# One of the four sums of weight blocks of a feed-forward group, formed by an accumulating transfer instead of VectorE

## The chip, the core and the metric

The kernel runs on one core of a Trainium2 chip. Its time is the device time of one execution in microseconds (us); lower is better. A core has five engines with queues of their own: TensorE (PE; PEld is its loading of weights), VectorE (DVE), ScalarE (ACT), GpSimd (POOL) and SyncE (SP). The last two also issue transfers here. All transfers run on the core's 16 DMA engines.

## What is computed

One step of a decoder layer for 512 prompt tokens and 8 sampled tokens, 520 columns in all, with a model width of 2048: a mixer, a cross-attention and a feed-forward part, each added to the running sum. The change touches the feed-forward part alone:

```python
hf = rmsnorm(x, w['g_ffn'])
x = x + (jnp.square(jax.nn.relu(hf @ w['w_up'])) @ w['w_down']).astype(x.dtype)
```

`w_up` is 2048 x 8192 and `w_down` 8192 x 2048, both float32. After it comes one more normalisation, and the output is written.

## The kernel before

Every float32 matrix product is made of three products of rounded parts: a weight block is cast to a high part (`whi`, ScalarE, L128), and what the rounding left is formed as a low part (`wlo`, VectorE, L129); the activations are split in the same way. A weight block is a tile of 128 x 1024 float32 values, 512 KB. `whi` and `wlo` have three buffers each.

The work is a list of jobs, each with one block of weights. `run_jobs` (L163) gives every job's loads out five jobs ahead (`FETCH`), forms and splits its weights two jobs ahead (`w_split`), and then issues its matmuls. A scheduler with priorities sets the final order of the instructions on each engine; each engine then works its queue in order.

The feed-forward part replaces eight block products by seven (a scheme of Strassen's kind). `quad_jobs` makes the seven jobs of a group, P1, P2, P6, P5, P7, P3, P4 in this order (`ORDER`). A group has four blocks of weights, A11, A12, A21 and A22, and each block is 512 KB. From them four more blocks are formed on VectorE, all by `tt` (L1222):

- S3 = A11 - A21, for P7, formed with P1's weights;
- S1 = A21 + A22, for P5, formed with P6's weights and written over A21;
- S2 = S1 - A11, for P6, written over A11;
- A12 - S2, for P3, written over S2.

P1 multiplies A11, P2 multiplies A12 and P4 multiplies A22. `fetch0` loads A11 and A21, `fetch1` loads A12 and A22, all of them on SP's queue. A11 and A12 stand in tiles named `wraw` (three buffers), A21, A22 and S3 in tiles of a pool with five buffers; the trace leaves numbers out of names, so that A21 and A22 both read as `A` there, and S3 as `S`.

There are 63 groups: 31 of the up-projection (`up_quad`; its first block of columns is multiplied plainly), whose results go through the squared ReLU and are stored, split, to `hc`, 910 KB twice for each group; and 32 of the down-projection (`down_quad`), in eight rounds of four groups. Each round reads 28 blocks of hidden values (`ha`, 260 KB each) on SP's queue, fetched ahead. A result of a product is added from PSUM to the running sum X by VectorE. The last four groups of the down-projection have another order (`LATE_ORDER`: P1, P6, P5, P7, P3, P2, P4), and squares of the finished columns are summed beside them. After the last product the sums are scaled and stored; POOL multiplies some of them (L1430).

GpSimd's queue carries loads and stores of the mixer and of the attention until 1200 us, and then nothing but these multiplications at the end.

Of the kernel before, what the change touches and what calls it, by code (L numbers as in the profile page):

```python
# [12 lines left out]
ALU = mybir.AluOpType  # L13
# [32 lines left out]
def tile_trunk(ctx: ExitStack, tc: tile.TileContext, a, o):  # L46
    nc = tc.nc
    V, S, PE, G = nc.vector, nc.scalar, nc.tensor, nc.gpsimd
# [15 lines left out]
    def nm(s):  # L64
        uid[0] += 1
        return f"{s}_{uid[0]}"
# [13 lines left out]
    def mm_tile():  # L80
        return late.get("mm", pmm).tile([P, 2, 512], F32, tag="mm", name=nm("mm"))
# [23 lines left out]
    def w_raw(src):  # L105
        raw = wpool.tile([P, 8, P], F32, tag="wraw", name=nm("wraw"))
        load(raw, src)
        return raw
# [1093 lines left out]
    def quad_jobs(srcs, acts, nacc, evac, order=None):  # L1202


        q, ps = {}, {}

        def raw2(name, src=None):
            t = late["sb"].tile([P, 8, P], F32, tag="wq", name=nm(name), bufs=5)
            if src is not None:
                load(t, src)  # L1210
            return t

        def fetch0():
            q["A11"] = w_raw(srcs[0])
            q["A21"] = raw2("A21", srcs[2])

        def fetch1():
            q["A12"] = w_raw(srcs[1])
            q["A22"] = raw2("A22", srcs[3])

        def tt(out, u, v, op):
            V.tensor_tensor(out=out, in0=u, in1=v, op=op)  # L1222
            return out

        def form(p):
            if p == "P1":
                q["S3"] = tt(raw2("S3"), q["A11"], q["A21"], ALU.subtract)
                return q["A11"]
            if p == "P2":
                return q["A12"]  # L1230
            if p == "P6":
                q["S1"] = tt(q["A21"], q["A21"], q["A22"], ALU.add)
                q["S2"] = tt(q["A11"], q["S1"], q["A11"], ALU.subtract)
                return q["S2"]
            if p == "P3":
                return tt(q["S2"], q["A12"], q["S2"], ALU.subtract)
            return q[dict(P5="S1", P7="S3", P4="A22")[p]]

        def mm(p, wh, wl):
            acc = ACC[p]  # L1240
            if acc not in ps:
                ps[acc] = mm_tile()
            new = p in ("P1", "P2", "P5")
            blocks = acts(p)
            per = 8 // nacc
            for c in range(nacc):
                out = ps[acc][:, c, 0:HT]
                for k in range(per):
                    x = blocks[k]
                    j = c * per + k  # L1250
                    for wi, (w, b) in enumerate(((wh, 0), (wh, 1), (wl, 0))):
                        PE.matmul(out, w[:, j, :], x[:, b], start=(new and k == 0 and wi == 0),  # L1252
                                  stop=(p == LAST[acc] and k == per - 1 and wi == 2),
                                  skip_group_check=True)

        js = []
        for i, p in enumerate(order or ORDER):
            js.append(dict(fetch=(fetch0, fetch1, lambda: None)[min(i, 2)], form=lambda p=p: form(p),
                           cost=0.5, mm=lambda wh, wl, p=p: mm(p, wh, wl),
                           post=lambda p=p: evac(p, ps[ACC[p]])))  # L1260
        return js
# [349 lines left out]
```

## Time and profile before

| what | value |
|---|---|
| median of 3 runs | 2697.18 us (2695.01 to 2697.83) |
| the profiled execution | 2695.61 us, of it 2693.5 us from the first to the last instruction |
| granted TensorE clock, mean | 0.997 of full speed |
| bytes moved by transfers | 512.41 MB, mean 190 GB/s |
| feed-forward groups of seven products | from about 1407 us to 2678 us |

Shares and rows below belong to the profiled execution. A row of a timeline gives the start in us from the span's start, the duration in us, the engine, the line of the program, the operation, the tile written and the tiles read with their shapes, and a count; in brackets at its end, where there are any, stand the idle time of the engine ahead of it and what ended that. A row of busy time by stretch gives the stretch, its length, the busy us (and instructions) of PE, PEld, DVE, ACT and POOL, the granted TensorE clock, the DMA share and GB/s. A DMA share is the mean busy share of the 16 DMA engines. Queue q0 carries the transfers that POOL issues, q1 those of SP.

### The profile page before, as it was taken

The numbers are of one execution on the slowest core, as the hardware profiler recorded it, in microseconds if no ns is written. First come the engines' busy times: TensorE is split into PE (matmuls) and PEld (weight loads), VectorE is DVE, ScalarE is ACT, GpSimd is POOL, SyncE is SP. The second block draws the span as 40 slices with busy tenths as digits, with TensorE's granted clock in tenths as the row PEclk, the third lists the DMA queues.
The fourth block names the chain that finished last, engine by engine and source line by source line (L and its number), as shares of the span: only waits on it lengthen the run. The fifth ranks groups of instructions, "written<-read, shape, count | busy, mean of one in ns | idle before, by whom it ended". The sixth has DMA issues, their size and how long they took to land.

```text
span 2693.5 us, 52716 instructions
## 1 busy us (share of the span) xinstructions
PE 2664.7 (99%) x21586; PEld 2628.1 (98%) x21586; DVE 2052.9 (76%) x3447; ACT 1219.4 (45%) x1653; POOL 152.1 (6%) x288
## 2 busy tenths in 40 slices
PE   9999999999999999999999999999999999999997
PEld 9999999999999998989999999999999999999997
DVE  6786686853345567875559899999999898898898
ACT  5646355542233135444445555555554333333344
POOL 0011010000001322210000000000000000000001
PEclk9999999999999999999999999999999999999999
DMA  5364353534435777876566656656569766556542
GB/s 202 105 189 138 119 166 104 171 95 139 138 130 197 259 269 248 277 244 203 183 213 213 229 186 203 203 186 205 202 213 337 239 214 220 171 169 206 206 133 89
DMA packets 225923, 512.41 MB, mean 190 GB/s; under 512 B 25502, under 2 KB 91710, under 8 KB 225682
## 3 DMA queue, kind: packets, MB, share of 16 engines
q1 hardware_dynamic: 205074, 441.92, 49.3%
q0 software_dynamic: 20608, 67.13, 7.4%
q8 instruction: 170, 2.79, 0.4%
q14 instruction: 71, 0.58, 0.1%
HBM read 416.16 MB, written 92.94 MB: 189 GB/s over the span
## 4 chain that ended last, share of the span: by engine, by line
PE 92%; DVE 3%; DMA 2%; ACT 1%; issue 1%; POOL 0%; SPq 0%; POOLq 0%; ACTq 0%; DVEq 0%
PE mm L1252 46%; PE mm L201 36%; PE aux L220 2%; PE mm L981 2%; PE mm L1012 2%; DMA wraw<-in_w_mv 1%; PE mm L1296 1%; DVE wlo L129 1%; DMA wraw<-in_w_mk 1%; DVE wlo L145 0%; PE aux L728 0%; ACT whi L128 0%; DMA out_rh<-hs 0%; PE aux L657 0%; ACT whi L137 0%
## 5 line engine op out<-in xcount | busy, mean ns | idle before, releaser
L128 ACT CAST whi<-wraw 128x1024 fp32r<-128x1024 f32 x396 | 416.0, 1050 | 807.4 <-PE mm L1252 376.4
L1252 PE MATMUL mm<-ha,whi 128*128 128x260 f32 x3584 | 643.7, 283 | 1.6 <-ACT whi L128 1.0
L129 DVE TENSOR_TENSOR wlo<-wraw,whi 128x1024 fp32r<-128x1024 f32 x396 | 484.2, 1223 | 198.7 <-ACT whi L128 196.0
L1252 PEld LDWEIGHTS mm<-ha,whi 128*128 128x128 f32 x3584 | 551.0, 188 | 2.4 <-ACT whi L128 1.2
L1252 PE MATMUL mm<-ha,wlo 128*128 128x260 f32 x1792 | 505.1, 282 | 0.6 <-DVE wlo L129 0.6
L1252 PE MATMUL mm<-ta,whi 128*128 128x260 f32 x1984 | 359.1, 283 | 0.0
L1252 PEld LDWEIGHTS mm<-ha,wlo 128*128 128x128 f32 x1792 | 337.0, 188 | 1.0 <-DVE wlo L129 1.0
L1252 PEld LDWEIGHTS mm<-ta,whi 128*128 128x128 f32 x1984 | 305.3, 188 | 0.0
L1252 PE MATMUL mm<-ta,wlo 128*128 128x260 f32 x992 | 280.1, 282 | 0.0
L1252 PE MATMUL mm<-fa,whi 128*128 128x260 f32 x1488 | 270.3, 283 | 0.0
L201 PE MATMUL mm<-xh,whi 128*128 128x260 f32 x1280 | 264.0, 287 | 0.0
L201 PE MATMUL mm<-xl,whi 128*128 128x260 f32 x1280 | 259.5, 284 | 0.0
L201 PE MATMUL mm<-xh,wlo 128*128 128x260 f32 x1280 | 257.7, 282 | 0.0
L1252 PEld LDWEIGHTS mm<-fa,whi 128*128 128x128 f32 x1488 | 229.2, 188 | 0.0
L137 ACT CAST whi<-wraw 128x1024 fp32r<-128x1024 f32 x100 | 105.0, 1050 | 256.3 <-PE mm L201 92.3
L128 ACT CAST whi<-A 128x1024 fp32r<-128x1024 f32 x126 | 132.2, 1049 | 185.9 <-PE mm L1252 125.5
L1252 PE MATMUL mm<-fa,wlo 128*128 128x260 f32 x744 | 210.0, 282 | 0.0
L1361 DVE TENSOR_TENSOR X<-mm,X 128x260 f32<-128x260 f32 x448 | 170.9, 422 | 40.5 <-PE mm L1252 39.4
L201 PEld LDWEIGHTS mm<-xh,whi 128*128 128x128 f32 x1280 | 198.4, 188 | 1.3
L201 PEld LDWEIGHTS mm<-xh,wlo 128*128 128x128 f32 x1280 | 198.1, 189 | 0.2
L201 PEld LDWEIGHTS mm<-xl,whi 128*128 128x128 f32 x1280 | 197.8, 189 | 0.3
L1252 PEld LDWEIGHTS mm<-ta,wlo 128*128 128x128 f32 x992 | 186.7, 188 | 0.0
(397 smaller groups left out, 5249.0 us busy)
## 6 DMA issues: line engine op xcount, KB each, us to landing
ha<-hc SPq DMA_DIRECT2D x224, 260.0 KB
wraw<-in_w_in SPq DMA_DIRECT2D x80, 512.0 KB
wraw<-in_w_up SPq DMA_DIRECT2D x66, 512.0 KB
wraw<-in_w_down SPq DMA_DIRECT2D x64, 512.0 KB
A<-in_w_down SPq DMA_DIRECT2D x64, 512.0 KB
A<-in_w_up SPq DMA_DIRECT2D x62, 512.0 KB
hc<-hhi SPq DMA_DIRECT2D x32, 910.0 KB
hc<-r SPq DMA_DIRECT2D x32, 910.0 KB
```

Of the source, the lines that this page charges most:

```text
L128: S.copy(hi, raw)
L129: V.tensor_tensor(out=lo, in0=raw, in1=hi.bitcast(F32), op=ALU.subtract)
L137: S.copy(hi, raw)
L201: PE.matmul(ps[:, hf, 0:HT], w[:, j, :], x[:, HALF[hf]], start=(k == 0 and wi == 0), stop=(k == n - 1 and wi == 2))
L220: PE.matmul(out, u, v, start=first and i == 0, stop=last and i == 2)
L981: PE.matmul(box["ps"], w[:, i, :], x, start=(k == 0 and wi == 0), stop=(k == KB - 1 and wi == 2))
L1012: PE.matmul(box["ps"][:, i], x[:, ms], w[:, j], start=(k == 0 and wi == 0), stop=(k == KB - 1 and wi == 2))
L1252: PE.matmul(out, w[:, j, :], x[:, b], start=(new and k == 0 and wi == 0), stop=(p == LAST[acc] and k == per - 1 and wi == 2), skip_group_c ...
L1296: PE.matmul(ps[:, hf, 0:HT], w[:, j, :], x[hf][:, b], start=(kp == 0 and j == 0 and wi == 0), stop=(kp == 1 and j == 7 and wi == 2))
L1361: V.tensor_tensor(out=x, in0=c, in1=x, op=ALU.add)
```

## The change

S1 is no longer an addition on VectorE. Once S3 has been formed, GpSimd issues a transfer that reads A22 from HBM and adds it to A21 in SBUF; S1 is the same tile as before. The load of A22 on SP's queue stays as it is, because P4 multiplies A22 itself.

```diff
         def form(p):
             if p == "P1":
                 q["S3"] = tt(raw2("S3"), q["A11"], q["A21"], ALU.subtract)
+                q["S1"] = q["A21"]
+                G.dma_start(q["S1"], srcs[3], accum_op=ALU.add)
                 return q["A11"]
             if p == "P2":
                 return q["A12"]
             if p == "P6":
-                q["S1"] = tt(q["A21"], q["A21"], q["A22"], ALU.add)
                 q["S2"] = tt(q["A11"], q["S1"], q["A11"], ALU.subtract)
                 return q["S2"]
```

VectorE's order in an early group of the up-projection, before, from S3 to S2 (`S3_2285` is the S3 of this group, `A21_2274` and `A22_2279` are its blocks, `wraw_2273` is A11 and then S2; L1327 to L1335 work on the results, L1280 on the hidden values):

```order
L1222 TENSOR_TENSOR S3_2285_16868<-wraw_2273_16764,A21_2274_16766 128x1024
L1327 TENSOR_TENSOR r_2269_16727<-mm_2272_16737,r_2269_16727 128x260
L129 TENSOR_TENSOR wlo_2276_16769<-S3_2261_16634,whi_2275_16768 128x1024
L1269 SCALAR_TENSOR_TENSOR r_2269_16727<-r_2269_16727,rssf_2211_16250 128x260
L1280 TENSOR_TENSOR r_2245_16493<-r_2245_16493,hhi_2277_16772 128x1820
L129 TENSOR_TENSOR wlo_2281_16808<-wraw_2249_16530,whi_2280_16807 128x1024
L1222 TENSOR_TENSOR A21_2274_16766<-A21_2274_16766,A22_2279_16804 128x1024
L129 TENSOR_TENSOR wlo_2284_16838<-A22_2255_16570,whi_2283_16837 128x1024
L129 TENSOR_TENSOR wlo_2287_16871<-wraw_2273_16764,whi_2286_16870 128x1024
L1335 TENSOR_TENSOR r_2269_16727<-r_2269_16727 128x260
L1222 TENSOR_TENSOR wraw_2273_16764<-A21_2274_16766,wraw_2273_16764 128x1024
```

The same piece of VectorE's order with the change:

```order
L1222 TENSOR_TENSOR S3_2285_16868<-wraw_2273_16764,A21_2274_16766 128x1024
L1328 TENSOR_TENSOR r_2269_16727<-mm_2272_16737,r_2269_16727 128x260
L129 TENSOR_TENSOR wlo_2276_16769<-S3_2261_16634,whi_2275_16768 128x1024
L1270 SCALAR_TENSOR_TENSOR r_2269_16727<-r_2269_16727,rssf_2211_16250 128x260
L1281 TENSOR_TENSOR r_2245_16493<-r_2245_16493,hhi_2277_16772 128x1820
L129 TENSOR_TENSOR wlo_2281_16808<-wraw_2249_16530,whi_2280_16807 128x1024
L129 TENSOR_TENSOR wlo_2284_16838<-A22_2255_16570,whi_2283_16837 128x1024
L129 TENSOR_TENSOR wlo_2287_16872<-wraw_2273_16764,whi_2286_16871 128x1024
L1336 TENSOR_TENSOR r_2269_16727<-r_2269_16727 128x260
L1222 TENSOR_TENSOR wraw_2273_16764<-A21_2274_16766,wraw_2273_16764 128x1024
```

The addition that wrote A21 is gone, and all else stands in the same order; the last row, S2, reads what the transfer leaves in A21. Over the whole program 63 such rows leave VectorE; of the rest a handful change places with a neighbour.

POOL's order at the end of the attention, before (the last loads, then the end of the kernel, L1430):

```order
L864 DMA kv_1977_14113<-in_V 128x512
L864 DMA kv_1978_14114<-in_V 128x512
L1430 ISA
L1430 TENSOR_TENSOR y_3962_31546<-X_3019_23807,rf_3955_31520 128x260
L1430 TENSOR_TENSOR y_3963_31550<-X_3045_24048,rf_3955_31520 128x260
```

And with the change:

```order
L864 DMA kv_1977_14113<-in_V 128x512
L864 DMA kv_1978_14114<-in_V 128x512
L1229 DMA A21_2182_16080<-in_w_up 128x1024
L1229 DMA A21_2250_16532<-in_w_up 128x1024
L1229 DMA A21_2274_16766<-in_w_up 128x1024
L1229 DMA A21_2298_17000<-in_w_up 128x1024
L1229 DMA A21_2322_17234<-in_w_up 128x1024
```

63 transfers, 31 of `w_up` and 32 of `w_down`, now stand between the attention's loads and the multiplications at the end. On SP's queue no transfer is added or removed; in some groups a weight load trades places with a neighbouring load.

## Rows read from the trace of the kernel before

**Rows 1.** The page, busy time (share of the span), instructions.
```profile
PE 2664.7 (99%) x21586; PEld 2628.1 (98%) x21586; DVE 2052.9 (76%) x3447; ACT 1219.4 (45%) x1653; POOL 152.1 (6%) x288
```

**Rows 2.** Busy time by stretch (columns as told above): up-projection, end.
```profile
1700.00:1850.00 150.00, 150.00 (x1254) 150.00 (x1253) 136.63 (x172) 81.05 (x97) 0.00 (x0) 1.00 0.61 205
...
2600.00:2693.00 93.00, 79.46 (x645) 77.68 (x644) 80.68 (x143) 43.84 (x73) 8.40 (x12) 0.95 0.29 98
```

**Rows 3.** Waits of TensorE, 1400 to 2640 us: total, times, longest.
```profile
PE mm L1252 <- ACT whi L128: 1.0, 1, 1.0
PE mm L1252 <- DVE X L1361: 0.5, 1, 0.5
PE mm L1252 <- DVE wlo L129: 0.4, 1, 0.4
```

**Rows 4.** Timeline of VectorE, one up group: S3, S1, P1's low half, S2, P2's, P6's.
```profile
1694.70 1.22 DVE L1222 TENSOR_TENSOR S<-wraw,A 128x1024 f32<-128x1024 f32 x1
...
1700.75 1.22 DVE L1222 TENSOR_TENSOR A<-A,A 128x1024 f32<-128x1024 f32 x1
...
1704.28 1.23 DVE L129 TENSOR_TENSOR wlo<-wraw,whi 128x1024 fp32r<-128x1024 f32 x1 [1.17 <-ACT whi L128]
...
1705.76 1.22 DVE L1222 TENSOR_TENSOR wraw<-A,wraw 128x1024 f32<-128x1024 f32 x1
...
1707.57 1.22 DVE L129 TENSOR_TENSOR wlo<-wraw,whi 128x1024 fp32r<-128x1024 f32 x1
...
1710.07 1.23 DVE L129 TENSOR_TENSOR wlo<-wraw,whi 128x1024 fp32r<-128x1024 f32 x1 [0.57 <-ACT whi L128]
```

**Rows 5.** Groups of POOL by line: busy us, mean ns of one.
```profile
L864 POOL DMA_DIRECT2D kv<-in_V x64 | 34.5, 539 | 29.0 <-DVE od L900 13.5 <-DVE sc L893 7.2 <-DMA kv<-in_V 3.2
```

**Rows 6.** Timeline of VectorE, one down group: S3, S2, P2's low half.
```profile
2319.19 1.23 DVE L1222 TENSOR_TENSOR S<-wraw,A 128x1024 f32<-128x1024 f32 x1
...
2330.42 1.22 DVE L1222 TENSOR_TENSOR wraw<-A,wraw 128x1024 f32<-128x1024 f32 x1
...
2332.23 1.22 DVE L129 TENSOR_TENSOR wlo<-wraw,whi 128x1024 fp32r<-128x1024 f32 x1
```

**Rows 7.** Timeline of VectorE, one of the last four groups: S3, S2.
```profile
2623.27 1.22 DVE L1222 TENSOR_TENSOR S<-wraw,A 128x1024 f32<-128x1024 f32 x1
...
2634.39 1.22 DVE L1222 TENSOR_TENSOR wraw<-A,wraw 128x1024 f32<-128x1024 f32 x1
```

**Rows 8.** Timeline of ScalarE: P5's cast in both groups, P2's at a handover.
```profile
1711.89 1.05 ACT L128 CAST whi<-A 128x1024 fp32r<-128x1024 f32 x1 [0.88 <-PE mm L1252]
...
2336.73 1.05 ACT L128 CAST whi<-A 128x1024 fp32r<-128x1024 f32 x1 [1.82 <-PE mm L1252]
...
2371.11 1.05 ACT L128 CAST whi<-wraw 128x1024 fp32r<-128x1024 f32 x1 [1.82 <-PE mm L1252]
```

**Rows 9.** Transfers issued 940 to 946 us: count, size, median us to landing.
```profile
kv<-in_K POOLq DMA_DIRECT2D x3, 256.0 KB, 3.7
```

**Rows 10.** Transfers issued 1047 to 1060 us.
```profile
kv<-in_K POOLq DMA_DIRECT2D x8, 256.0 KB, 7.2
```

**Rows 11.** Busy time by stretch: those loads, the first handover, a later one.
```profile
1047.00:1064.00 17.00, 16.57 (x84) 13.68 (x83) 12.89 (x36) 6.68 (x10) 7.52 (x14) 1.00 1.00 372
2010.00:2130.00 120.00, 118.96 (x993) 118.64 (x992) 109.42 (x151) 49.37 (x49) 0.00 (x0) 1.00 0.94 325
2337.00:2371.00 34.00, 34.00 (x286) 34.00 (x286) 30.63 (x44) 12.34 (x12) 0.00 (x0) 1.00 0.95 339
```

**Rows 12.** The page, DMA queue of SP: packets, MB, share of 16 engines.
```profile
q1 hardware_dynamic: 205074, 441.92, 49.3%
```

**Rows 13.** Busy time by stretch, the same up group.
```profile
1696.00:1698.00 2.00, 2.00 (x19) 2.00 (x18) 2.00 (x4) 1.85 (x2) 0.00 (x0) 1.00 0.00 0
1698.00:1700.00 2.00, 2.00 (x19) 2.00 (x19) 2.00 (x2) 0.76 (x2) 0.00 (x0) 1.00 0.90 307
```

**Rows 14.** Timeline of SP, a later handover: the load of A12.
```profile
2357.58 0.33 SPq L107 DMA_DIRECT2D wraw<-in_w_down  x1
```

## The prediction

> **What bounds the kernel now.** I read the share of busy time first, then busy time by stage, then the waits of TensorE, then the engines' timelines over single groups of seven products, and last the transfers. TensorE is busy for 99% of the span [rows 1]. By stage it is busy for all 150 us of a stretch of the up-projection, beside 136.63 us of VectorE and a DMA share of 0.61; only in the last 93 us does it stand still for longer, and most of that is the final normalisation and the store of the output [rows 2]. From 1400 to 2640 us its named waits come to 1.0 + 0.5 + 0.4 = 1.9 us in all [rows 3]. So the feed-forward stage runs at the pace of the matmuls. VectorE is nearly full there, but it runs ahead of TensorE by the depth of the buffers, and nothing waits for it.
>
> **What the change takes away.** 63 additions of 1.22 us on VectorE (the middle row of [rows 4] is one): 76.9 us of busy time. What hides them is TensorE. With them gone, VectorE comes sooner to its next wait, for the cast of a block, which itself waits for TensorE to give back a buffer (the 1.17 us ahead of 1704.28 grow) [rows 4]. Gain: at most the 1.9 us of [rows 3], and likely none of it, since those three waits do not follow an addition. I take 0.
>
> **What it adds.** 63 transfers on POOL's queue. Each can begin only when S3 has been read off the old A21, and the same 512 KB of A22 are read from HBM a second time: the plain load on SP stays, since P4 multiplies A22 itself. So 33 MB more are read from HBM, and the sum's destination is read and written in SBUF. Issuing one of the 256 KB transfers took POOL 539 ns [rows 5]; POOL does nothing else in this stage, the next sum's transfer comes a group (20 us) later, and the twelve multiplications that end the kernel stand behind the last. POOL's queue I cost at nothing.
>
> **What waits for it.** VectorE now waits for the transfer just ahead of S2 = S1 - A11, and everything behind S2 on VectorE is held with it. The cover has two parts.
>
> First, S3 to S2. In an up group S3 ends at 1694.70 + 1.22 = 1695.92 and S2 begins at 1705.76: 9.84 us [rows 4]. In a down group 2319.19 + 1.23 = 2320.42 to 2330.42: 10.0 us [rows 6]. In one of the last four groups, with their other order, 2623.27 + 1.22 = 2624.49 to 2634.39: 9.9 us [rows 7].
>
> Second, what is queued behind S2. The low half of P2's block ends at 1707.57 + 1.22 = 1708.79 [rows 4], and TensorE takes up P2 only at 1711.89. That I read from the casts: there are three buffers, so the cast for the product two places later begins when P2 does [rows 8]. So 3.1 us more may pass before TensorE stands still. In a down group it is 2336.73 - (2332.23 + 1.22) = 3.3 us [rows 6, 8]. A delay of that size does not pile up from group to group: VectorE has 0.57 us, 1.17 us and the 1.22 us saved, 2.96 us in each group, to catch up. In the last groups VectorE is full, so there I count no second part.
>
> So the cover is **12.9 us** in the 31 up groups, 13.3 us in the down groups and 9.9 us in the last ones, from the end of S3 to the landing.
>
> **How long the transfer takes.** No row shows an adding transfer. From below: a plain 256 KB load on POOL's queue among little other traffic landed in 3.7 us [rows 9], as if size and addition cost nothing. From above: the same kind of load in a stretch where the DMA share was 1.00 landed in 7.2 us [rows 10, 11]; four times that, for twice the bytes with a destination that is read as well, is 28.8 us, if all of it were bytes. Between them: 512 KB cost all 16 engines together 0.493 x 2693.5 us / 441.92 MB x 0.524 MB = 1.58 us [rows 12]. An adding transfer reads 1 MB where the row of 3.7 us read 256 KB, three quarters of a megabyte more, 2.4 us. Quiet: 0.5 + 3.7 + 2.4 = 6.6 us. Against a full queue, with half of the engines' turns: 0.5 + 7.2 + 2 x 2.4 = 12.5 us. In an up group the transfer begins near 1696.5, when the DMA engines are idle, and meets the group's own stores and loads from 1698 on [rows 13]. I take **9 us**, between the two: it lands at about 1704.9, before S2. Both values lie inside 12.9 us, so the term is 0 with either; the quiet value also holds for most down groups and the last ones.
>
> One rule of the Trainium skill speaks against the change: SBUF — State Buffer, section "SBUF: two separate sides". A transfer issued from GpSimd has its descriptors written by GpSimd, and these writes stand still while a VectorE operation holds the port pair that the two share. By the rule the transfer would start only when VectorE pauses, and the sum would be the third rival's. The page's section "Who interferes with whom" says that the two-tensor form, which is what VectorE runs in this stage, has no such mode. No run here shows an adding transfer beside a full VectorE.
>
> **What it does to the other transfers.** A group's adding transfer reads 512 KB from each of two places: 2 x 1.58 = 3.2 us of all engines [rows 12] in 20 us, which adds 0.16 to a share of 0.61 [rows 2]: room enough. It is tight only where the next hidden blocks are fetched, 34 us at 0.95 in each of the later handovers and 120 us at 0.94 at the first [rows 11]. In the later ones a weight load issued at 2357.58 [rows 14] is first cast at 2371.11 [rows 8]: 13.5 us. If it landed as quickly as the load of [rows 9], 9.8 us are to spare; if it landed only as the burst ends, near 2371, none. I take 8 us of room against a delay of some 5 us, so 0.
>
> **The sum.** 2695.61 us (the profiled execution: span 2693.5 us and 2.1 us around it), less 0, plus 0. The median of the three runs stands 1.57 us above that execution, so the forecast is **2697.2 us**, no change. A measurement of this kernel can tell some 0.2%, 5.4 us, from no change; the forecast's own range is that, 2692 to 2702.
>
> **The rivals.**
>
> 1. Slower: the transfer lands after the cover in the up groups, where it shares the engines with two stores of 910 KB and three loads [rows 13]. It decides from 12.9 us after S3 on. At 14 us the cost is 1.1 us x 31 = 34 us, **2731 us**; at the upper bound, (28.8 - 12.9) x 63, about 1000 us. For it: the loaded estimate is already 12.5 us. Against it: the head start in idle engines, and that 7.2 us belongs to a stretch with several such loads in flight, where here there is one.
> 2. Slower: the full stretches at the handovers. Two transfers of 3.2 us meet 0.05 x 34 = 1.7 us of room, so loads fall 4.7 us behind; at the first, six of them, 19 us against 7, 12 us behind. Weight loads then come after their cast. With 1 us lost at each of the seven and 5 us at the first: 12 us, **2709 us**; at most 7 x 4.7 + 12 = 45 us. Against it: the 9.8 us to spare above.
> 3. Slower: VectorE holds up the start. In an up group it pauses first at 1703.1 (1704.28 less 1.17) [rows 4]; 9 us later is 1712.1, 6.3 us late for S2 and 3.2 us beyond the cover: 31 x 3.2 = 100 us, **2797 us**. Against it: VectorE runs two-tensor forms alone here.
> 4. Faster by more than 5.4 us: there are 1.9 us of waits to remove [rows 3], so this needs something that no row shows.
>
> That the addition does not leave VectorE can be excluded: its 63 rows are gone from VectorE's order and stand in POOL's.
>
> **How the numbers follow.** Forecast 0.68; late landing 0.17; handovers 0.10; VectorE's hold 0.03; faster 0.02. So faster 0.02, same 0.68, slower 0.30. The range goes from 2692, the lower edge of no change, to 2731, the first rival at 14 us; it leaves out about half of that rival, the third and most of the fourth, 0.13 in all.
>
> **What would show it.** Right: no rows of VectorE that add A22 to A21, VectorE's busy time 77 us lower, 63 more transfers of 512 KB on POOL with a median landing near 9 us, S2 waiting for them seldom and by less than 3 us, and TensorE's waits in the stage still near 2 us. Rival 1 shows as idle time ahead of S2 in each up group, released by the transfer, with TensorE waiting for low halves; rival 2 as TensorE's waits only near the handovers; rival 3 as landings that follow VectorE's pauses. The forecast is wrong if a landing passes 13 us in the ordinary groups.

## The result and the profile with the change

| | before | with the change |
|---|---|---|
| median | 2697.51 us (14 runs, 2695.01 to 2699.45) | 2703.29 us (14 runs, 2700.9 to 2709.56) |
| ratio | | 1.0023, 95% interval 1.0016 to 1.003 |
| profiled execution, its span | 2695.61 us, 2693.5 us | 2700.9 us, 2699.1 us |

The change costs 0.23%, 5.8 us. That is inside the range and just past the bound of no change. All ratios leave out executions over 1.5% above the fastest of the same kernel; there was one, of 8946.21 us, in the run below in which VectorE adds in 5 groups, with a mean granted clock of 0.285.

Busy time by engine [rows 1]:

```profile
PE 2667.2 (99%) x21586; PEld 2630.2 (97%) x21586; DVE 1989.0 (74%) x3384; ACT 1218.9 (45%) x1653; POOL 206.9 (8%) x351
```

VectorE has 63 instructions fewer, and 63.9 us less busy time where the prediction said 77. Added up one by one, the durations of its instructions do fall by 77.8 us. The rest is overlap: an instruction that follows another at once starts some 0.08 us before that one's end, and busy time counts this stretch once. With the additions gone more of the others come after a pause (879 instead of 793), and 13.9 us less of them overlap. TensorE is busy for 2.5 us longer with the same instructions, which points to its clock.

The two stretches of [rows 2], and the crowded one of [rows 11]:

```profile
1700.00:1850.00 150.00, 150.00 (x1254) 150.00 (x1254) 128.23 (x164) 81.07 (x97) 6.08 (x7) 1.00 0.81 229
2600.00:2693.00 93.00, 84.61 (x688) 82.75 (x686) 82.23 (x146) 45.73 (x75) 10.20 (x14) 0.99 0.34 99
2010.00:2130.00 120.00, 116.19 (x949) 115.71 (x948) 99.27 (x139) 47.56 (x48) 5.20 (x6) 0.97 1.00 340
```

In an ordinary stretch TensorE is as full as before, and the DMA share went from 0.61 to 0.81. The end holds more of TensorE's work only because everything arrives there 5 us later. At the first handover, from the up- to the down-projection, the share is 1.00, TensorE lost 2.8 us of busy time, and the mean granted clock is 0.97.

TensorE's waits from 1400 to 2640 us [rows 3], and VectorE's for transfers in the same part:

```profile
PE mm L1253 <- DVE X L1362: 3.7, 2, 3.1
PE mm L1253 <- ACT whi L128: 0.7, 1, 0.7
```

```profile
DVE wraw L1222 <- DMA A<-in_w_down: 3.8, 3, 1.8
...
DVE X L1362 <- DMA X<-dx: 3.4, 1, 3.4
```

S2 (`wraw`, L1222) waited for the new transfer in three of 63 groups, none of the up-projection. One addition to X waited 3.4 us for a plain load of X. The new transfers by themselves, from the rows of `A` on POOL, with POOL's DMA queue (before, it took 7.4%):

```profile
L1229 POOL DMA_DIRECT2D A<-in_w_down x32: 857/867/891, 2018.7 to 2650.4; - x32
L1229 POOL DMA_DIRECT2D A<-in_w_up x31: 856/867/908, 1379.0 to 1998.5; - x31
...
DMA to landing us min/median/max: 5.3/5.7/11.0
```

```profile
q0 software_dynamic: 29680, 100.16, 14.7%
```

A transfer lands in 5.7 us in the median, in 7.8 us for those of `w_down` alone. It takes (0.147 x 2699.1 - 0.074 x 2693.5) / 63 = 3.1 us of all 16 engines.

### The profile page after: what moved, and what is told of

Read it like the earlier page. It is cut to its first block, busy times and chain, and to the rows that moved or that the text cites. A ratio compares the mean times of both kernels' runs of the same rounds, so it can differ in the third digit from the quotient of the medians.

```text
span 2699.1 us, 52928 instructions
## 1 busy us (share of the span) xinstructions
PE 2667.2 (99%) x21586; PEld 2630.2 (97%) x21586; DVE 1989.0 (74%) x3384; ACT 1218.9 (45%) x1653; POOL 206.9 (8%) x351
## 4 chain that ended last, share of the span: by engine, by line
PE 92%; DVE 2%; DMA 2%; issue 2%; ACT 1%; POOL 0%; SPq 0%; POOLq 0%; DVEq 0%; ACTq 0%
PE mm L1253 44%; PE mm L201 36%; PE mm L981 3%; PE aux L220 2%; PE mm L1012 2%; PE mm L1297 1%; DVE wlo L129 1%; PE aux L728 1%; PE aux L657 0%; DMA hc<-r 0%; DMA out_rh<-hs 0%; PE aux L661 0%; ACT whi L128 0%; PE aux L654 0%; PE aux L252 0%
```

## Where the time went

The chain that ended last, of before and then of the change, in order of time (start, duration, what):

```profile
1407.05 635.54 PE mm L1252 x5302
2042.62 1.05 ACT whi L128
2043.86 564.23 PE mm L1252 x4715
```

```profile
1407.00 610.15 PE mm L1253 x5092
2017.14 5.02 DMA ha<-hc
2022.16 12.60 DMA hc<-r
2034.83 5.22 DMA X<-dx
2040.08 0.43 DVE X L1362
...
2042.71 5.37 PE mm L1253 x23
2048.10 1.05 ACT whi L128
2049.18 564.23 PE mm L1253 x4715
```

Both reach the seven-product groups at 1407 us, and both run without a break for the same 564.23 us after the first handover, through all seven later ones. Between them the change lost (2049.18 - 1407.00) - (2043.86 - 1407.05) = **5.37 us, once**. Below, "the stage" is the time from the start of that first run of matmuls to the end of the last: 2043.86 + 564.23 - 1407.05 = 1201.04 us before, 1206.41 us with the change. It leaves out the attention, which wanders by some us from one execution to the next.

What happened there, on TensorE (its two breaks) and by stretch:

```profile
2042.71 0.80 PE L1253 MATMUL mm<-ha,whi 128*128 128x260 f32 x2 [3.12 <-DVE X L1362]
2049.18 0.48 PE L1253 MATMUL mm<-ha,whi 128*128 128x260 f32 x2 [0.69 <-ACT whi L128]
```

```profile
2039.00:2043.00 4.00, 0.88 (x6) 0.67 (x6) 2.91 (x6) 2.08 (x2) 0.00 (x0) 0.89 1.01 385
2043.00:2048.00 5.00, 5.00 (x24) 5.00 (x24) 3.19 (x3) 0.58 (x1) 0.87 (x1) 0.50 1.05 371
```

TensorE stood still for 3.12 + 0.69 us, where before it stood for 1.04 us, so 2.8 us are stops. The other 2.6 us go with the clock: after the long stop the granted clock was 0.50, its lower level of 1.2 GHz, for five us, in which 24 matmuls ran instead of some 42. Before, the stop of 1.04 us was followed by no such stretch.

The queue of SP ahead of it, before and then with the change:

```profile
2022.33 7.09 SPq L1353 DMA_DIRECT2D ha<-hc  x7
2031.35 2.14 SPq L1381 DMA_DIRECT2D X<-dx  x4
```

```profile
2023.72 9.11 SPq L1354 DMA_DIRECT2D ha<-hc  x7
2034.83 2.27 SPq L1382 DMA_DIRECT2D X<-dx  x4
```

X is issued 3.5 us later, and VectorE waits 3.4 us for it, so it had hardly any room. An estimate says the same: 5.22 us from issue to landing (the chain of the change), put after 2031.35, gives 2036.57, and before, VectorE's first addition to X began at 2036.63.

## The experiments

The theory after the first reading: the whole loss is made at the first handover, because the adding transfers' share of full DMA engines makes X late. Its rivals: a loss too thin to see, spread over 63 groups; and the waits of S2 in later down groups. All ratios are against runs of the kernel before on the same chip. The stage is read from one profiled execution of each kernel; in the three that lost nothing it agrees to 0.03 us (1201.04, 1201.02 and 1201.03 us).

| run | median, us | ratio (95%) | the stage, us, against 1201.04 |
|---|---|---|---|
| VectorE adds in 2 groups | 2699.74 | 1.0008 (0.9999 to 1.0017) | 1202.82, +1.78 |
| transfer in 2 groups alone | 2700.6 | 1.0015 (1.0007 to 1.0024) | 1204.87, +3.83 |
| X's first loads on POOL | 2703.19 | 1.0023 (1.0013 to 1.0033) | 1207.88, +6.84 |
| copy without a wait in 2 groups | 2699.18 | 1.0007 (0.9998 to 1.0016) | +0.43 (to the last break) |
| VectorE adds in 5 groups | 2698.16 | 1.0003 (0.9994 to 1.0012) | 1201.02, -0.02 |
| plain load in place of the sum | 2699.24 | 1.001 (1.0001 to 1.0019) | 1203.10, +2.06 |

### Take the transfer away at the handover, and keep it there alone

`quad_jobs` got a switch for each group; with it off, VectorE adds as before:

```diff
             if p == "P1":
                 q["S3"] = tt(raw2("S3"), q["A11"], q["A21"], ALU.subtract)
-                q["S1"] = q["A21"]
-                G.dma_start(q["S1"], srcs[3], accum_op=ALU.add)
+                if moved:
+                    q["S1"] = q["A21"]
+                    G.dma_start(q["S1"], srcs[3], accum_op=ALU.add)
...
             if p == "P6":
+                if not moved:
+                    q["S1"] = tt(q["A21"], q["A21"], q["A22"], ALU.add)
```

First run: `moved=i != 31` in `up_quad`, `moved=(ck, g) != (0, 0)` in `down_quad`.

> 61 transfers as in the changed kernel; only the last up group and the first down group form S1 by VectorE's addition. Theory (all of the loss is made once, at the first handover, by the engine time of the two transfers issued there at 1998 and 2019 us): X's first loads go out near 2031 us again, TensorE's long stop there goes from 3 us to 1 us, the granted clock stays at 1.00, and the time is that of the kernel before, 2697.5 us within 1.5 us. Rival 1 (the loss is spread over the 63 groups, too little in each to be seen as a named wait): some 61/63 of it stays, about 2703. Rival 2 (VectorE's three waits of 3.8 us for adding transfers in down groups cost it): these groups are left as they are, so about 2703 too.

Second run: the opposite conditions, so that two transfers are left in all.

> The kernel before with the transfer in two groups alone, the last up group and the first down group. Theory: the whole loss is back, 2703 us within 1.5 us, with the stop of 3 us and the lower clock near 2040 us. Rivals 1 and 2 (spread over the groups, or the waits of later down groups): 2/63 of 5.8 us or nothing, so 2697.5 us.

Two transfers of 63 bring back 3.83 of 5.37 us, with a stop of 2.48 us and the clock at 0.72 from 2044 to 2048. Without them 1.78 us stay. So the loss does sit at the first handover, but taking these two transfers away does not end it. The chain of the first run names what is left:

```profile
2043.47 1.14 DVE S L1222
...
2045.25 9.31 DMA A<-in_w_down
...
2056.56 1.14 DVE wlo L129
2057.74 2.90 PE mm L1256 x22
...
2061.57 549.83 PE mm L1256 x4595
```

In this run it is the sum itself, in the second down group. In the crowd the transfer takes 9.31 us from issue. And its cover is short there: VectorE still has the last up group's hidden values to finish, S3 ends at 2044.61, and S2 comes up only 6 us later (it starts at 2054.66 after 3.95 us of waiting), not 10 us as in [rows 6]. TensorE then stops for 0.35 and 0.94 us.

In the kernel with the change this step did not happen. There the same sum landed 9.8 us after S3, and S2 waited for it:

```profile
2055.99 1.23 DVE L1222 TENSOR_TENSOR wraw<-A,wraw 128x1024 f32<-128x1024 f32 x1 [1.47 <-DMA A<-in_w_down]
```

but TensorE, held up by X a few us earlier, has no stop after 2049.18 that the waits name until 2626.93. So its whole loss is made by the late X, and the late sum shows only where X is in time.

### Only the traffic, or only the queue

A plain copy of the same block, HBM to HBM, in the two groups, with VectorE adding everywhere:

```diff
+                elif spare is not None:
+                    G.dma_start(spare, srcs[3])
```

> The kernel before, VectorE adding in all groups; in the last up group and the first down group POOL also issues a plain transfer of the same 512 KB block from HBM to an unused place in HBM, for which nothing waits. Theory (engine time is what costs, not the wait for the sum): X's loads go out late again and most of the loss is there, 2701 to 2704 us, less if a plain copy takes less of the engines than the 3.1 us of an adding transfer. Rival (the wait for the sum, or the addition at the destination, costs): 2697.5 us within 1.5 us.

It costs hardly anything: X goes out 625.04 us after the stage's start, against 624.30 before and 627.17 with two adding transfers. So the expectation fell on this point: it is not traffic of 512 KB as such. But the copy isn't the adding transfer's traffic either, it goes in larger packets (32 each, by q0's 20672 against 20608; an adding one has 144) and never touches SBUF.

X's first four loads moved off SP's queue:

```diff
-                    load(X[n], dx[1][n])
+                    (stream_load if g == 0 else load)(X[n], dx[1][n])
```

> All 63 transfers, but the first four loads of X are issued by POOL, so that they no longer stand behind the hidden blocks' loads on SP's queue. Theory (what is late is X, because SP issues it after 19 loads and stores that the full DMA engines hold up): X lands before 2036 us, the stop at 2040 us goes, perhaps with the 1 us that the kernel before had there: 2696 to 2698 us. Rival (the DMA engines are full whatever the order, so hidden blocks or weights come late in X's place): a stop of TensorE of about the same length released by ha or by a weight block's cast, and 2701 to 2705 us.

The rival was right. X no longer waits, but A21 of the second down group lands late in its place, and TensorE stops for 6.0 us:

```profile
2048.86 1.22 DVE L1222 TENSOR_TENSOR S<-wraw,A 128x1024 f32<-128x1024 f32 x1 [5.30 <-DMA A<-in_w_down]
```

With the DMA engines full, another order only chooses what is late.

### All of the first down round

`moved=i != 31` and `moved=ck > 0`: 58 transfers are left.

> 58 transfers; VectorE forms S1 in the last up group and in all four groups of the first down round. Theory (the loss is made in two steps of the same crowded stretch, 1998 to 2065 us: the engine time of the first two transfers makes X late, and the transfer of the second down group lands 9.3 us after its issue and holds S2 by 4 us): without these five transfers nothing is left, 2697.5 us within 1 us, TensorE's stop near 2040 us is the 1 us that the kernel before has. Rival (some of the loss comes from the other 58): 2698.5 to 2700 us, with named waits of TensorE elsewhere.

The chain, and the only wait for the sum in the stage:

```profile
1410.43 635.54 PE mm L1256 x5302
2047.23 564.22 PE mm L1256 x4715
```

```profile
DVE wraw L1222 <- DMA A<-in_w_down: 0.8, 1, 0.8
```

Both runs of matmuls are those of the kernel before to 0.01 us. So 58 transfers cost nothing, and nothing is spread thinly: with these five gone, the whole loss is gone. That 3.83 and 1.78 us add up to nearly 5.37 us is chance. The last three of the five are issued after X has gone out (the first of them at 2046.83), and in the kernel with the change they stopped nothing. There X went out 0.66 us later than with two transfers alone (627.83 us after the stage's start), the stop was 3.12 instead of 2.48 us, and the clock stayed down for longer; why X was later still, these runs don't tell.

### What the addition costs in the transfer

All 63 transfers, but without `accum_op`: the additions of A21 and A22 are left out, S1 is A22.

```diff
-                G.dma_start(q["S1"], srcs[3], accum_op=ALU.add)
+                G.dma_start(q["S1"], srcs[3])
```

> All 63 transfers, each a plain load of A22 over A21: the additions are left out, so S1 is A22 alone. Order, waits and places are those of the changed kernel. Theory (the addition at the destination is what makes a transfer dear, 3.1 us of all engines against 1.58 us for a plain one): a transfer takes 1.5 to 2 us of the engines, lands in 4 to 5 us in the up groups, and the loss shrinks to 1 to 3 us, 2698.5 to 2700.5 us. Rival (any transfer that POOL issues at these places and that S2 waits for costs as much): 2702 to 2704 us and landings of 5 to 6 us as before.

```profile
L1229 POOL DMA_DIRECT2D A<-in_w_down x32: 527/528/544, 2021.6 to 2650.0; - x32
...
q0 software_dynamic: 29680, 100.16, 11.8%
```

Same bytes and packets, but 0.53 us of POOL instead of 0.87, 1.9 us of all engines instead of 3.1, landing in 4.5 us (`w_up`) and 5.3 us (`w_down`) instead of 5.7 and 7.8, and 2.06 us lost instead of 5.37; X goes out 625.84 us after the stage's start, 1.5 us late instead of 3.5. The theory holds here: the addition is what makes a transfer dear. Whether X is late for the engines' time alone, or for the way in which an adding transfer's packets take turns with SP's, the runs don't tell apart.

### How much cover an ordinary group has

The main term of the prediction, 12.9 us from S3's end to the landing, was never reached, but two down groups of the kernel with the change came near it: their sums held S2 until 10.5 and 11.7 us after S3's end, and TensorE waited for nothing. The later of the two, S3 and S2:

```profile
2204.11 1.23 DVE L1222 TENSOR_TENSOR S<-wraw,A 128x1024 f32<-128x1024 f32 x1
...
2217.06 1.23 DVE L1222 TENSOR_TENSOR wraw<-A,wraw 128x1024 f32<-128x1024 f32 x1 [1.79 <-DMA A<-in_w_down]
```

To reach the bound in up groups, the transfer is issued later in most of them, and the first down round is as in the run with 58 transfers. First by small multiplications on POOL, six and then fourteen:

```diff
+                    if late_by:
+                        t = late["sb"].tile([P, 2, P], F32, tag="jk", name=nm("jk"), bufs=1)
+                        for _ in range(late_by):
+                            G.tensor_tensor(out=t, in0=q["A21"][:, 0:2], in1=q["S3"][:, 0:2], op=ALU.mult)
                     G.dma_start(q["S1"], srcs[3], accum_op=ALU.add)
```

> As the run with VectorE's addition in the first round, and in 28 of the up groups POOL first does six small multiplications that read A21 and S3 (results unused), some 4 us, before it issues the transfer. Landing some 10 to 11 us after S3's end, more than the 9.84 us to S2 and less than the cover of 12.9 us. Theory (the cover has a second part, 3.1 us, because TensorE works ahead of VectorE): S2 is held by up to 1 us and TensorE waits for nothing: the time of the run without the delay, 2697.5 us within 1.5 us. Rival (no second part, each us of S2's delay is paid): 28 x 0.5 to 1 us, 2712 to 2725 us.

> As the run before it, with fourteen multiplications, some 10 us, ahead of the transfer: it lands some 16 us after S3's end. Theory (12.9 us are covered): (16 - 12.9) x 28 = 87 us lost, 2785 us, in general 28 x (landing - 12.9 us), plus what the clock loses after each stop. Rival 1 (cover of 9.84 us only): 28 x 6.2 = 174 us, 2871 us. Rival 2 (delays add up from group to group, or more cover than counted): above 2871 or below 2740 us.

2899.02 us and 3033.7 us: far more than expected, because the delays were far longer. Six multiplications took 9.2 us, not 4, and VectorE's beside them went from 1.22 to 1.75 us. So the delay was next hung on a cast of ScalarE, with one multiplication of 128x64 that reads it: P4's cast, P1's, and P3's.

```diff
+                if held:
+                    t = late["sb"].tile([P, 64], F32, tag="jk", name=nm("jk"), bufs=1)
+                    G.tensor_tensor(out=t, in0=q["A21"][:, 0, 0:64], in1=late["hi"][:, 0, 0:64].bitcast(F32),
+                                    op=ALU.mult)
```

> As the run with VectorE's addition in the first round, but in 26 of the up groups POOL does one small multiplication (128x64, result unused) ahead of the transfer, which needs the cast of the former group's P4; that cast ends some 5.4 us after S3. So the transfer should be issued about 6 us after S3's end and land 11.5 to 12 us after it: S2 is held by about 2 us in each group. Theory (cover of 12.9 us: behind S2 another 2.5 to 3 us pass before TensorE lacks anything): TensorE waits for nothing, 2698 us within 2 us, while VectorE's waits for the transfer sum up to some 50 us. Rival (what S2 is late, TensorE is late): 26 x 2 = 52 us and more, 2750 us or above.

> The same, with the transfer behind the cast of P1's block, which ends 8.3 us after S3: issued about 8.7 us after S3's end, landing 14.4 to 16.6 us after it (5.7 to 8 us from issue). Theory (cover of 12.9 us): TensorE stops 1.5 to 3.7 us in each of the 26 groups, 39 to 96 us in all, released by the sum into r that stands behind S2 on VectorE; with what the lowered clock adds (in the two runs with POOL's multiplications a stop cost 1.3 to 1.5 times its length) 2750 to 2840 us. Rival (the cover ends at S2, 9.84 us): 4.6 to 6.8 us each, 120 to 177 us of stops, 2855 us or more.

> The same as the run with the transfer behind the cast of P4, with VectorE's and ScalarE's order unchanged, but the transfer stands behind the former group's P3 cast, one cast earlier: issued some 4.4 us after S3's end and, at 5.7 to 9.3 us from issue, landing 10.1 to 13.7 us after it. Theory (cover of 12.9 us; in the run behind P4's cast TensorE stopped 3.5 us in each group for a landing at 16.3 us, which is 16.3 - 12.9 = 3.4): VectorE waits for the transfer in nearly all 26 groups, up to 3.8 us each and some 50 us in sum, and TensorE stops 0 to 0.8 us in each: 2698 us if the landing is below 12.9 us, at most 2698 + 26 x 0.8 x 1.5 = 2730 us. Rival (TensorE loses what S2 is late): 26 x 2 us and more, 2750 us or above.

2854.44, 2830.73 and 2843.29 us. The landings behind P4's and P3's casts again came later than planned, 15 to 17 us after S3, so the two cases meant to lie inside the cover lay outside. But they measure it. One group of the run behind P4's cast, on VectorE (S3, the last work ahead of S2, S2), POOL and TensorE:

```profile
1700.86 1.22 DVE L1222 TENSOR_TENSOR S<-wraw,A 128x1024 f32<-128x1024 f32 x1
...
1711.44 0.42 DVE L1343 TENSOR_TENSOR r<-r 128x260 f32<-128x260 f32 x1
1718.40 1.23 DVE L1222 TENSOR_TENSOR wraw<-A,wraw 128x1024 f32<-128x1024 f32 x1 [6.54 <-DMA A<-in_w_up]
```

```profile
1707.51 1.35 POOL L1230 TENSOR_TENSOR jk<-A,whi 128x64 f32<-128x64 f32 x1 [24.24 <-ACT whi L128]
1709.26 0.88 POOL L1234 DMA_DIRECT2D A<-in_w_up  x1 [0.41 <-POOL jk L1230]
```

```profile
1720.45 0.47 PE L1260 MATMUL mm<-fa,whi 128*128 128x260 f32 x2 [2.52 <-DVE r L1346]
1721.49 0.58 PE L1260 MATMUL mm<-fa,wlo 128*128 128x260 f32 x1 [0.57 <-DVE wlo L129]
```

S3 ends at 1702.08, VectorE is free for S2 at 1711.86 (9.8 us, as in [rows 4]), the sum lands at about 1718.4, 16.3 us after S3. TensorE stops for 2.52 + 0.57 = 3.1 us. So 13.2 us were covered in this group; the prediction said 12.9. Over all 26 groups, TensorE's waits and VectorE's for the sum:

```profile
PE mm L1260 <- DVE r L1346: 80.5, 26, 4.4
PE mm L1260 <- DVE wlo L129: 10.7, 26, 0.6
```

```profile
DVE wraw L1222 <- DMA A<-in_w_up: 185.1, 26, 8.4
```

(185.1 - 80.5 - 10.7) / 26 = 3.6 us of each wait pass without harm to TensorE; the same three sums of the run behind P3's cast, 176.7, 72.2 and 10.6 us, give 3.6 us too. The prediction had 3.1 us. The first part is shorter there than in [rows 4], 9.3 us from S3's end until VectorE is free for S2 instead of 9.84, so that the cover is 12.9 us in the mean of both runs (11.6 to 13.7 us from group to group). What TensorE lacks first is not P2's low half. It is a place for results: the sum into r (L1339 of the kernel with the change) stands behind S2 too, and TensorE waits for it before the low half. The run behind P1's cast can't be set beside these: there the order on VectorE changed as well, S2 came behind the sum into r, and TensorE stopped 79.6 us in all for a copy on ScalarE that stood behind the cast of S2. Its time lies in the range that the theory gave, but not by the theory's path.

A stop costs more than its length. Against the 2698.16 us of the run with 58 transfers, the run behind P4's cast lost (2854.44 - 2698.16) / 26 = 6.0 us for each group with 3.5 us of stops, the one behind P3's cast 5.6 us for 3.2 us; the two runs with 28 groups lost 7.2 us for 4.6 us and 12.0 us for 9.1 us. The difference is 2.4 to 2.9 us in all four; in the run behind P1's cast it is 2.0 us (5.1 us for 3.1 us), in that with two transfers alone 1.6 us. It goes with the clock after the stop; in the run with fourteen multiplications, after a stop of 9.4 us:

```profile
1705.00:1710.00 5.00, 4.73 (x21) 4.43 (x22) 5.00 (x8) 2.36 (x4) 0.00 (x0) 0.50 0.00 0
```

Stops of 1.0 to 1.2 us left it at 1.00 in the kernel before and in four of the runs above, but of the three shortest stops for the sum into r in the run behind P3's cast, 1.16, 1.22 and 1.45 us, the first and the last were followed by 0.50.

The last run was to hold the transfer back by a small store on POOL's queue instead:

> As the run before it, but what holds the transfer back to the former group's P3 cast is no multiplication (it took 2.4 to 4.5 us there, as it went on until VectorE paused) but a small store of 8 KB that POOL issues ahead of it in 26 up groups and that reads that cast. The transfer is then issued some 3.1 us after S3's end, between the group's two stores and ahead of its loads, and lands 9 to 12 us after it. Theory (cover of 12.9 us, of which 9.8 to S2): VectorE waits for the transfer by up to 2 us in some groups, TensorE for nothing, 2698 us within 1.5 us, in the stage the 1201 us of the run with VectorE's addition in the first round. Rival (TensorE loses what S2 is late): up to 26 x 2 us, visible as TensorE's waits released by the sum into r: 2710 to 2775 us.

2696.58 us, ratio 0.9996 (0.9987 to 1.0005), the stage 1201.03 us. But it does not test the expectation: the scheduler put the store behind the transfer (1696.51 us the transfer, 1699.00 us the store), so nothing was held back. It stands as a second run of the kernel with 58 transfers (and 26 small stores), with the same answer. That a sum landing between 10 and 13 us costs nothing in an up group was therefore not run; it follows from the 3.6 us above, and the two down groups with 10.5 and 11.7 us bear it out.

No version beats both kernels. VectorE's freed time buys nothing in the stage, with the five transfers or without.

## Why the prediction was right and wrong

**What bounds the kernel, and the gain of 0.** Right. Taking 58 additions, 70.8 us, from VectorE left TensorE's runs of 635.54 and 564.22 us as they were when the handover was spared.

**The landing of 9 us.** Too long: 5.7 us in the median, below even the quiet value of 6.6 us. The estimate's error had no effect. Its loaded value of 12.5 us was not idle, though: issued after the group's stores, the same transfer took 9.3 us and 9.9 us in the median (the runs behind P4's and P3's casts). The likely reason for the early landing is that it is issued just ahead of them.

**The engines' time of 3.2 us.** Right, 3.1 us; a DMA share of 0.61 + 0.16 = 0.77 was worked out, 0.81 measured. That it came from counting two reads of 512 KB is luck in part: the plain load of the same bytes takes 1.9 us, not 1.58.

**The cover of 12.9 us in up groups.** Right, 12.9 us in the mean of two runs, but in part by luck: the first part came out 0.5 us shorter, the second 0.5 us longer, and the sum into r is late before P2's low half is. In the first down round the cover is not 13.3 us: in the run that spared X a sum that held S2 until 10.05 us after S3's end already stopped TensorE. A down group from 2319 us was taken to stand for all.

**"I take 8 us of room against a delay of some 5 us, so 0."** This step failed, and only at the first handover. The room belongs to weight loads of a later handover. At the first, the first loads of X stand on SP's queue behind the hidden blocks, with less than 0.1 us to spare by the estimate above; they came 3.5 us late. At the seven later ones the step held: not one stop.

**The rivals.** The second one is what happened, in its place and near its size at the first handover (5 us taken, 5.4 us in the stage), with 0 instead of 1 us at each later one; but X was late, not the weight loads that it named, and half of the size is the clock, which it did not count. The first rival's mechanism, a late sum, cost 1.8 us in one group where X was in time, and nothing in the kernel with the change. Its price counts no clock; whether a stop of 1.1 us brings the lower clock differed from stop to stop. The third is excluded: beside a VectorE busy for 128.23 of 150 us the transfers of up groups landed in 5.7 us, and none was late.

**The forecast.** 2697.2 us was forecast and 2703.29 us measured; no change had 0.68, slower by over 0.2% had 0.30. Of its signs, the 63 rows, the 63 transfers and S2's three waits of at most 1.8 us came out as said; the median landing did not, and TensorE's waits in the stage came to 4.4 us instead of about 2. The handovers deserved more than 0.10: the estimate of 12 us behind at the first stood in the text, and who would be late there was worked out for weights alone.

## What to carry to other kernels

When work moves from an engine to transfers, look for the one stretch where the DMA engines are already full, and list everything on the queues there with its landing and its first reader, not the loads of one kind; 58 of 63 transfers were free here. Two made X late, and three more had to go because a late sum then took X's place. A cover measured in one group holds for groups that look like it, not for the first after a change of phase, where the engines still work off the former one. And a stop of TensorE is to be priced with the clock after it: here 1.6 to 2.9 us on top of a stop of 2 us or more, and nothing or little after most stops of about 1 us.

## What the runs showed of the hardware that was not expected

- An adding transfer of 512 KB takes 3.1 us of all 16 engines and 0.87 us of POOL's issue; a plain one in the same place 1.9 us and 0.53 us.
- A multiplication of 128x64 on POOL can last until VectorE pauses. In the run behind P3's cast it took 2.3 to 4.5 us, and 24 of the 26 end about 0.18 us after the start of a pause of VectorE; the other two end between two of VectorE's operations, the second of which took 1.35 and 1.33 us instead of 1.22. Of the 24, one took 2.81 us at 1694.80 and one 4.51 us at 1718.95, and both end within 0.2 us of the end of an unbroken row of two-tensor work on VectorE:

```profile
1697.66 1.22 DVE L130 TENSOR_TENSOR wlo<-A,whi 128x1024 fp32r<-128x1024 f32 x1 [0.24 <-ACT whi L129]
...
1722.06 1.22 DVE L130 TENSOR_TENSOR wlo<-A,whi 128x1024 fp32r<-128x1024 f32 x1
```

```profile
1694.80 2.81 POOL L1231 TENSOR_TENSOR jk<-A,whi 128x64 f32<-128x64 f32 x1 [21.37 <-ACT whi L129]
...
1718.95 4.51 POOL L1231 TENSOR_TENSOR jk<-A,whi 128x64 f32<-128x64 f32 x1 [20.07 <-ACT whi L129]
```

1694.80 + 2.81 = 1697.61, inside the pause of 0.24 us that ends at 1697.66; 1718.95 + 4.51 = 1723.46, just after VectorE's 1722.06 + 1.22 = 1723.28. The Trainium skill, SBUF — State Buffer, section "Who interferes with whom", has it that a VectorE operation with two inputs in SBUF and a GpSimd operation that reads SBUF contend; these rows agree. POOL's transfers, which the change issues at the same places, show none of it: POOL issued each in 0.86 to 0.91 us.
